# A later place for the value products and keys prepared by pairs, in a two-layer trunk with latent attention

## The chip, the cores and the metric

The kernel runs on one core of a Trainium2 chip. The metric is the device time of one execution in microseconds (us), as the median of several runs. The profile is that of one execution, taken by the hardware profiler; its times are counted from the first instruction of the program. Engines are called as the profile calls them: PE is TensorE's matmul and PEld its weight load, DVE is VectorE, ACT is ScalarE, POOL is GpSimd, and SP is the engine whose queue issues nearly all DMAs.

## The reference

The input is 512 tokens of 1024 channels, with 16 learned meta tokens put in front (528 rows in all). Two layers follow. Each normalizes the residual stream, projects it by one wide matrix into eight parts, and mixes tokens in two parallel ways: causal pooling over four windows, and attention with 8 heads. A head has 64 channels without position and 32 channels with rotary position (rope); the 32 rope channels of the key are the same for all heads before the key is normalized, and the norm then gives every head its own factor per token.

```python
q = (c_q @ w_q_b).reshape(B, L, N_HEADS, QK_HEAD_DIM)
kv = (c_kv @ w_kv_b).reshape(B, L, N_HEADS, QK_NOPE_DIM + V_HEAD_DIM)
k_nope, v = kv[..., :QK_NOPE_DIM], kv[..., QK_NOPE_DIM:]
k_pe = jnp.broadcast_to(k_rope_raw[:, :, None, :], (B, L, N_HEADS, QK_ROPE_DIM))
k = jnp.concatenate([k_nope, k_pe], axis=-1)
q = rmsnorm(q, g_qn)
k = rmsnorm(k, g_kn)
...
o = causal_block_attention(q, k, v)          # softmax(q k^T / sqrt(96)) v, causal
...
y_mla = (o_mla * jax.nn.silu(z_mla)) @ mla_w_up[l]
merged = jax.nn.sigmoid(g_pool) * y_pool + jax.nn.sigmoid(g_mla) * y_mla
h_res = h_res + merged @ w_out[l]
```

All is in float32, and the result has to hold float32 accuracy.

## The kernel before, in words

**Precision.** TensorE works on a shorter float32 form (fp32r). So each operand is split into a high part, which ScalarE makes by a copy (`act.activation(..., AF.Copy)`), and a low part, which VectorE makes by a subtraction. `split` (L294 to L296) does this for activations and `wload` (L196, L197) for weights. A product is three matmuls (L201 to L203): high by high, high by low, low by high.

**Two streams of work.** Activations are kept transposed, channels on partitions and the 528 tokens along the row. All weight products of both layers stand in one list, `plan`; `stream` (L210) walks it chunk by chunk (512 columns of weight, that is four tiles of 128 by 128) and yields after every six matmuls, with 6 x columns / 2.4 as its planned nanoseconds. Weights are loaded into `raw` (three buffers) by SP. The attention of a layer is written out by hand in `go` (L1084) and `head` (L784), and in its gaps `fill` (L282) draws from the stream as many planned nanoseconds as `FILL` says (2620 in layer 0, 2530 in layer 1), until `gm3` is done; the products gm4 to gm7 are kept for the end. `fill_now` draws a given amount at once, and `after` puts a piece of work (a closure) behind so many nanoseconds of drawn stream; `LAG` is 2000.

**Order of the work.** The framework plans at build time: it simulates a timeline (`schedule_with_timeline_sim=True`), takes for each engine the earliest piece in program order whose inputs are ready in the simulation, and so freezes one order per engine. On the chip each engine works its queue strictly in that order, and a DMA that has to wait stands in SP's queue ahead of all that follows. `behind` (L302) adds a true wait for another instruction; `newest` is the last matmul of the stream that has been written out.

**One head.** `prep(h)` makes the key and the query of a head. The key factors, one row per head in DRAM (`kdr`), were broadcast over 128 partitions by `spread_k` (L758), two heads ahead. VectorE multiplies 64 rows of the normalized key by them (L767), POOL the rope rows (L768), and `split` makes `kh` and `kl` (two buffers each). Even heads have their position-free rows on partitions 0 to 63 and rope on 64 to 95, odd heads have rope on 0 to 31 and the others on 64 to 127; the rest of the query is zero. The query's rope rows are copied into `qhl` by two DMAs (L781).

`head(h)` then computes scores of query tiles 1, 3 (in part) and 2 (L201 to L203 with output S), their row minimum on VectorE (L803), the exponentials on ScalarE (L810) and block transposes on VectorE (`turn`, L816). After a gap, `parts(prev)` splits the turned probabilities of the head before, and after another gap come the rest of tile 3 and tile 0 (L841), with the same steps. The transposed blocks go to DRAM by four DMAs (`pdr<-attD`, L868) and come back in order by one (`attE<-pdr`, L870; two buffers). The row sums go through DRAM too (L863, L871). For an odd head the 16 meta keys of two heads are turned and sent through DRAM into `racc` (L885, L887; one buffer).

`parts` (L890) splits `attE`: two activations of 128x640 into `th` and two subtractions in place. `pv` (L900) is the value product: four matmuls with the high part (L918) and four with the low part (L921) into one PSUM bank `o` (for the last head a bank of S), then ScalarE and VectorE add its two halves (L926, L927). For an odd head `part2` (L931) follows after two lags, for the last head after three: it adds the meta keys' part (L933), multiplies by the gate (L936, L937) and splits the result into `ogs`, from which the products mu0 to mu7 are made.

The loop over heads in `go` is: `head(h)`, gap, `prep(h+1)`, `pv` of head h-1, gap. After the loop come the meta tokens' own queries (layer 0), 2600 ns of stream, `parts` of head 7, 2600 ns more, its `pv`, and the rest of the stream up to `gm7`.

## Time and profile before

| what | value |
|---|---|
| median of 3 runs | 799.87 us (798.21 to 802.26) |
| the profiled execution, as timed | 800.05 us |
| its span, first to last instruction | 798.3 us |
| granted TensorE clock, mean over the span | 0.987 |
| busy: PE, DVE, ACT, POOL | 766.5, 553.7, 397.1, 166.4 us |
| heads of layer 0 and of layer 1, about | 172 to 326 us and 575 to 723 us |

A row of the groups reads: line, engine, operation, output<-inputs, partitions x elements and count, then busy time and the mean of one in ns, then the idle time of the engine just before and what ended it. A row of the waits reads: who waited, for whom, the total in us, how often, the longest. A row of a timeline or of the chain reads: start in us, length in us, engine, line. A row of an instruction group of one line has minimum, median and maximum in ns and the first and last start.

### The profile page before, as it was taken

The numbers are of one execution on the slowest core, as the hardware profiler recorded it, in microseconds if no ns is written. First come the engines' busy times: TensorE is split into PE (matmuls) and PEld (weight loads), VectorE is DVE, ScalarE is ACT, GpSimd is POOL, SyncE is SP. The second block draws the span as 40 slices with busy tenths as digits, with TensorE's granted clock in tenths as the row PEclk, the third lists the DMA queues.
The fourth block names the chain that finished last, engine by engine and source line by source line (L and its number), as shares of the span: only waits on it lengthen the run. The fifth ranks groups of instructions, "written<-read, shape, count | busy, mean of one in ns | idle before, by whom it ended". The sixth has DMA issues, their size and how long they took to land. (4 is left out here: it accounts for less than half of the span.)

```text
span 798.3 us, 14211 instructions
## 1 busy us (share of the span) xinstructions
PE 766.5 (96%) x5028; PEld 692.4 (87%) x5028; DVE 553.7 (69%) x1219; ACT 397.1 (50%) x868; POOL 166.4 (21%) x195
## 2 busy tenths in 40 slices
PE   9999999999898999999999999999998989889998
PEld 9999999999897998899997898887886767768887
DVE  5588677457788986684466486674567979868642
ACT  5755656445544654543354355564435555554321
POOL 2026204011112220052130262030112212211400
PEclk9999999999899999999999999999999999999999
DMA  7533233345555565424642332233455564573353
GB/s 266 170 103 103 69 100 107 96 142 160 163 157 165 150 172 171 124 99 141 182 137 92 109 93 78 96 96 118 148 165 152 143 190 145 158 222 121 106 185 105
DMA packets 74642, 109.76 MB, mean 138 GB/s; under 512 B 14358, under 2 KB 35222, under 8 KB 74572
## 3 DMA queue, kind: packets, MB, share of 16 engines
q1 hardware_dynamic: 74428, 108.61, 44.8%
q8 instruction: 39, 0.64, 0.3%
q14 instruction: 31, 0.25, 0.1%
q10 hardware_dynamic: 144, 0.26, 0.1%
HBM read 90.85 MB, written 15.86 MB: 134 GB/s over the span
## 5 line engine op out<-in xcount | busy, mean ns | idle before, releaser
L203 PE MATMUL mm<-hh,wlo 128*128 128x264 f32 (+2 forms) x1072 | 339.4, 319 | 3.5 <-DVE wlo L197 3.5
L201 PE MATMUL mm<-hh,whi 128*128 128x264 f32 (+2 forms) x1072 | 339.3, 318 | 0.8 <-ACT whi L196 0.8
L202 PE MATMUL mm<-hl,whi 128*128 128x264 f32 (+2 forms) x1072 | 338.6, 317 | 0.0
L197 DVE TENSOR_TENSOR wlo<-raw,whi 128x512 fp32r<-128x512 f32 (+2 forms) x242 | 175.0, 727 | 89.2 <-ACT whi L196 85.6
L196 ACT ACTIVATE whi<-raw 128x512 fp32r<-128x512 f32 (+2 forms) x242 | 144.1, 599 | 152.3 <-PE mm L202 124.3
L203 PEld LDWEIGHTS mm<-hh,wlo 128*128 128x128 f32 x1072 | 202.7, 190 | 17.2 <-DVE wlo L197 5.1
L201 PEld LDWEIGHTS mm<-hh,whi 128*128 128x128 f32 x1072 | 203.7, 190 | 14.7 <-ACT whi L196 1.3
L202 PEld LDWEIGHTS mm<-hl,whi 128*128 128x128 f32 x1072 | 203.6, 190 | 13.1
L296 DVE TENSOR_TENSOR attE<-attE,th 128x640 fp32r<-128x640 f32 x32 | 30.5, 972 | 39.8 <-ACT th L295 39.8
L295 ACT ACTIVATE th<-attE 128x640 fp32r<-128x640 f32 x32 | 21.9, 729 | 60.3 <-DMA attE<-pdr 60.3
L768 POOL TENSOR_TENSOR tmp<-kp,bc 64x528 f32<-64x528 f32 x16 | 25.5, 1592 | 85.3 <-PE mm L203 69.8
L813 POOL COPY pm<-cq 128x16 f32<-128x16 f32 x32 | 13.5, 423 | 141.4 <-ACT cq L810 140.6
L628 POOL TENSOR_TENSOR racc<-racc,tmp 128x264 f32<-128x264 f32 (+1 forms) x15 | 14.3, 957 | 135.3 <-ACT tmp L627 135.3
L803 DVE CUSTOM_DVE_ANT_0 S<-S,maskw,nqs 128x240 f32<-128x240 f32 (+4 forms) x80 | 37.6, 492 | 5.2 <-PE S L203 4.6
L993 POOL TENSOR_TENSOR tmp<-tmp,xb 128x264 f32<-128x264 f32 (+1 forms) x24 | 26.1, 1097 | 51.2 <-DVE tmp L991 45.9
L810 ACT ACTIVATE cq<-S,bia 128x400 f32<-128x400 f32 (+2 forms) x48 | 24.4, 511 | 21.8 <-DVE bia L803 14.1
L201 PE MATMUL mm<-cq,whi 128*128 128x264 f32 (+1 forms) x108 | 34.8, 322 | 0.0
L202 PE MATMUL mm<-th,whi 128*128 128x264 f32 (+1 forms) x108 | 34.6, 321 | 0.0
L201 PE MATMUL mm<-u,whi 128*128 128x264 f32 (+1 forms) x108 | 34.6, 320 | 0.0
L203 PE MATMUL mm<-cq,wlo 128*128 128x264 f32 (+1 forms) x108 | 34.5, 321 | 0.0
L202 PE MATMUL mm<-cq,whi 128*128 128x264 f32 (+1 forms) x108 | 34.5, 321 | 0.0
L203 PE MATMUL mm<-u,wlo 128*128 128x264 f32 (+1 forms) x108 | 34.5, 319 | 0.0
(295 smaller groups left out, 1334.5 us busy)
## 6 DMA issues: line engine op xcount, KB each, us to landing
raw<-win SPq DMA_DIRECT2D x143, 256.0 KB, 2.9
pdr<-attD SPq DMA_DIRECT2D x64, 160.0 KB, 3.0
attE<-pdr SPq DMA_DIRECT2D x16, 640.0 KB, 4.8
raw<-wout SPq DMA_DIRECT2D x32, 256.0 KB, 2.8
bc<-kdr SPq DMA_DIRECT2D x16, 264.0 KB, 3.7
raw<-wpu SPq DMA_DIRECT2D x16, 256.0 KB, 2.6
raw<-wmu SPq DMA_DIRECT2D x16, 256.0 KB, 2.6
raw<-wqb SPq DMA_DIRECT2D x12, 256.0 KB, 2.6
```

The lines of the kernel that those rows point to most:

```text
L196: act.activation(hi[:, :n], raw[:, :n], AF.Copy)
L197: dve.tensor_sub(lo[:, :n], raw[:, :n], hi[:, :n].bitcast(F32))
L201: first = pe.matmul(out, wh, xh, start=start, stop=False)
L202: pe.matmul(out, wh, xl, start=False, stop=False)
L203: newest[0] = pe.matmul(out, wl, xh, start=False, stop=stop)
L295: act.activation(hi[:, a:b], src, AF.Copy)
L296: return dve.tensor_sub(lo[:, a:b], src, hi[:, a:b].bitcast(F32))
L628: self.acc_last = gp.tensor_add(self.acc[:, a:b], self.acc[:, a:b], t[:, :b - a])
L768: gp.tensor_mul(kf[r0:r0 + 64, :], self.kp[r0:r0 + 64, :], bc[r0:r0 + 64, :])]
L803: return dve.tensor_tensor_reduce(out=sv, in0=sv, in1=mask, scale=nqs[:, i, h:h + 1], scalar=3e38, op0=ALU.add, op1=ALU.min, accum_out=bia ...
L810: act.activation(pv, sv, AF.Exp, scale=-1.0, bias=bia[:, i:i + 1], accum_out=rs[:, c:c + 1])
L993: gp.tensor_add(t[:, :b - a], t[:, :b - a], self.am[m][:, a:b])
```

## The change

It has four parts.

1. The value product of head h-1 moves from the end of the loop's pass h into the middle of `head(h+1)`, where `parts` was; `parts` of head h-1 moves to the end of pass h, after `prep(h+1)`. In the program `late` is the head whose parts are made and whose product is due, `prev` the one before that.
2. In `parts` the two high parts wait, by `behind`, for the stream's newest matmul at that place.
3. After the loop stand the product of head 6, then 9000 planned ns of stream (`TAIL`) instead of 2600, `parts` of head 7, 2600 ns and its product.
4. Keys: `keys(p)` multiplies and splits all 128 rows of a pair of heads at once, in the middle of the odd head before, with factors of two heads broadcast to 64 partitions each. The rope rows of four heads at a time are multiplied and split once per layer, in `k_factors`, for which the raw rope rows are copied to all four groups of 32 partitions in `kr_rest`. `prep` then puts a head's key together by DMA: the rope rows (two DMAs, for all heads) and, for even heads, the 64 position-free rows (two more) into the second buffer. The odd head's key is the pair's own buffer. Even heads use 96 partitions in the score products.

```diff
--- before.py
+++ after.py
@@ -53,6 +53,7 @@
 FILL = (2620.0, 2530.0)
 RESERVE = ("gm3", "gm3")
 LAG = 2000.0
+TAIL = (9000.0, 9000.0)
 SPL = 240
 RET = 12500.0
 WARM = 8
@@ -503,7 +504,8 @@
                 self.kraw = slot("kn3")
             t, kr = self.kp[:, a:b], self.kraw[:, a:b]
             behind(dve.tensor_mul(t, t, self.inv[:, a:b]), newest[0])
-            gp.tensor_copy(t[64:96, :], t[0:32, :])
+            for g in (32, 64, 96):
+                gp.tensor_copy(t[g:g + 32, :], t[0:32, :])
             q = next(self.half)
             made = act.activation(q[:, :b - a], t, AF.Square)
             self.stat(q[:, :b - a], a, b, C_KPE, made)
@@ -543,8 +545,17 @@
             newton(ny, na, nt)
             sp.dma_start(flat(kdr[self.l]), ny)
             self.bcs = {}
-            for h in range(2):
-                self.spread_k(h)
+            self.spread_k(0)
+            self.kr = []
+            for r in range(2):
+                bc = slot("bc", bufs=3)
+                sp.dma_start(bc, kdr[self.l][4 * r:4 * r + 4, :].unsqueeze(1).to_broadcast([4, 32, T]))
+                f = tmp()
+                dve.tensor_mul(f[:, :T], self.kp, bc)
+                t = slot(f"cq{4 + 2 * r}", F32R), slot(f"cq{5 + 2 * r}", F32R)
+                split(*t, f[:, :T], 0, T)
+                self.kr.append(t)
+            self.spread_k(1)
 
         def rope(self, out, src, a, b):
             n = b - a
@@ -753,33 +764,41 @@
                 self.smeta = self.smeta32[0:NM]
                 gp.memset(self.smeta32, 0.0)
 
-        def spread_k(self, h):
-            self.bcs[h] = bc = slot("bc", bufs=3)
-            sp.dma_start(bc, kdr[self.l][h:h + 1, :].partition_broadcast(P))
+        def spread_k(self, p):
+            self.bcs[p] = bc = slot("bc", bufs=3)
+            sp.dma_start(bc, kdr[self.l][2 * p:2 * p + 2, :].unsqueeze(1).to_broadcast([2, 64, T]))
+
+        def keys(self, p):
+            t = [(slot("kh", F32R, bufs=2), slot("kl", F32R, bufs=2)) for _ in range(2)]
+            self.ks[p] = t if p % 2 else t[::-1]
+            kf, bc = tmp()[:, :T], self.bcs.pop(p)
+            made = dve.tensor_mul(kf, self.kn[p], bc)
+            if p + 2 < H // 2:
+                self.spread_k(p + 2)
+            split(*self.ks[p][1], kf, 0, T)
+            return made
 
         def prep(self, h):
             p, odd = h // 2, h % 2
             n0, r0 = (64, 0) if odd else (0, 64)
-            kf = tmp()
-            bc = self.bcs.pop(h)
-            if h + 2 < H:
-                self.spread_k(h + 2)
-            made = [dve.tensor_mul(kf[n0:n0 + 64, :], self.kn[p][n0:n0 + 64, :], bc[n0:n0 + 64, :]),
-                    gp.tensor_mul(kf[r0:r0 + 64, :], self.kp[r0:r0 + 64, :], bc[r0:r0 + 64, :])]
-            kh, kl = slot("kh", F32R, bufs=2), slot("kl", F32R, bufs=2)
-            split(kh, kl, kf[:, :T], 0, T)
+            kd = self.ks[p][odd]
+            g0 = 32 * (h % 4)
             qh, ql = qhl[odd]
             x0 = self.x0
             src = self.qn[p][n0:n0 + 64, x0:T]
-            made.append(act.activation(qh[n0:n0 + 64, x0:T], src, AF.Copy))
+            made = act.activation(qh[n0:n0 + 64, x0:T], src, AF.Copy)
             if h == 0:
-                for ins in made:
-                    behind(ins, newest[0])
+                behind(made, newest[0])
             dve.tensor_sub(ql[n0:n0 + 64, x0:T], src, qh[n0:n0 + 64, x0:T].bitcast(F32))
-            g0 = 32 * (h % 4)
+            if odd == 0:
+                for d, f in zip(kd, self.ks[p][1]):
+                    sp.dma_start(d[0:64, :].bitcast(F32), f[0:64, :].bitcast(F32))
+            for d, f in zip(kd, self.kr[h // 4]):
+                sp.dma_start(d[r0:r0 + 32, :].bitcast(F32), f[g0:g0 + 32, :].bitcast(F32))
             for d, f in zip((qh, ql), self.qr[h // 4]):
                 sp.dma_start(d[r0:r0 + 32, x0:T].bitcast(F32), f[g0:g0 + 32, x0:T].bitcast(F32))
-            return kh, kl, qh, ql
+            m = P if odd else QK
+            return [t[0:m] for t in (*kd, qh, ql)]
 
         def head(self, h, kq, prev):
             kh, kl, qh, ql = kq
@@ -831,7 +850,9 @@
             turn(1)
             turn(2)
             self.gap()
-            self.parts(prev)
+            self.pv(prev)
+            if odd and h + 1 < H:
+                self.keys(h // 2 + 1)
             self.gap()
             sc = sct()
             s0, s4 = sc[:, 0:144], sc[:, 144:144 + T - SPL]
@@ -889,13 +910,14 @@
 
         def parts(self, prev):
             if prev is None:
-                return
+                return None
             h, got = prev
-            hi = wide()
-            f = got.bitcast(F32)
+            hi, f = wide(), got.bitcast(F32)
             for a in (0, NB * 64):
-                split(hi, got, f[:, a:a + NB * 64], a, a + NB * 64)
-            self.pt = hi, got
+                b = a + NB * 64
+                behind(act.activation(hi[:, a:b], f[:, a:b], AF.Copy), newest[0])
+                dve.tensor_sub(got[:, a:b], f[:, a:b], hi[:, a:b].bitcast(F32))
+            return h, hi, got
 
         def pv(self, prev, hosts=()):
             if prev is None:
@@ -914,7 +936,7 @@
             for j in range(4):
                 k0, n = block(j, j), 4 - j
                 st = block(j + 1, j) - k0 if n > 1 else 1
-                hi, lo = (t.rearrange("p (a s r) -> p s a r", a=4, s=NB)[:, k0:k0 + st * (n - 1) + 1:st] for t in self.pt)
+                hi, lo = (t.rearrange("p (a s r) -> p s a r", a=4, s=NB)[:, k0:k0 + st * (n - 1) + 1:st] for t in prev[1:])
                 chain(pe.matmul(o[:, P * j:512], vt[:, j, h, :], hi, start=j == 0, stop=j == 3))
                 for fn in hosts[2 * j:2 * j + 2]:
                     chain(fn())
@@ -1120,24 +1142,27 @@
             up("qn3")
             self.qk_stats()
             fill_now(2600)
+            self.ks = [None] * 4
+            behind(self.keys(0), newest[0])
             kq = self.prep(0)
             fill_now(2600)
             due[0] = None
-            prev = None
+            late = prev = None
             for h in range(H):
-                now = self.head(h, kq, prev)
+                now = self.head(h, kq, late)
                 self.gap()
                 if h + 1 < H:
                     kq = self.prep(h + 1)
-                self.pv(prev)
+                late = self.parts(prev)
                 prev = now
                 self.gap()
+            self.pv(late)
             if not self.last:
                 self.meta_queries()
+            fill_now(TAIL[self.l])
+            late = self.parts(prev)
             fill_now(2600)
-            self.parts(prev)
-            fill_now(2600)
-            self.pv(prev)
+            self.pv(late)
             up("gm7")
             flush()
             if not self.last:
```

## The prediction

> **What bounds the kernel now.** I read the page first, then TensorE's waits, then stretches of the two attention stages, then the chain that ended last. The page says that TensorE is the bound, with 798.3 - 766.5 = 31.8 us of idle time in the whole span:

> ```profile
> span 798.3 us, 14211 instructions
> ...
> PE 766.5 (96%) x5028; PEld 692.4 (87%) x5028; DVE 553.7 (69%) x1219; ACT 397.1 (50%) x868; POOL 166.4 (21%) x195
> ```

> The profiled execution took 800.05 us, so 1.75 us lie around the span; the median of the three runs is 799.87, 0.2 below it. The waits of TensorE (total, times, longest):

> ```profile
> PE o L918 <- ACT th L295: 15.7, 11, 3.6
> PE S L918 <- ACT th L295: 4.5, 2, 2.5
> PE mm L203 <- DVE wlo L197: 3.5, 4, 1.3
> PE mm L933 <- DMA racc<-mdr: 2.2, 2, 1.7
> ```

> So 15.7 + 4.5 = 20.2 us of idle time is the value product (L918) waiting for ScalarE's high part of the turned probabilities (L295). The next view has the attention stage of layer 0 and of layer 1, and below them the five stretches that follow the longest of these waits (columns: window; length and PE; PEld; DVE; ACT; POOL; granted clock; DMA share; GB/s):

> ```profile
> 172.00:326.00 154.00, 140.80 (x1075) 137.37 (x1075) 124.81 (x325) 79.58 (x202) 27.99 (x43) 0.96 0.54 159
> 575.00:723.00 148.00, 134.11 (x621) 107.15 (x620) 118.43 (x270) 75.56 (x176) 29.22 (x43) 0.98 0.58 164
> 216.50:222.30 5.80, 5.80 (x24) 5.51 (x25) 5.74 (x12) 3.75 (x12) 2.57 (x3) 0.50 0.18 58
> 259.90:263.30 3.40, 3.40 (x15) 3.00 (x14) 3.40 (x10) 2.16 (x9) 0.60 (x2) 0.50 0.33 100
> 321.30:324.70 3.40, 3.40 (x14) 3.30 (x15) 3.40 (x8) 1.60 (x5) 0.77 (x1) 0.50 0.13 48
> 618.30:621.70 3.40, 3.40 (x10) 2.51 (x9) 3.40 (x9) 2.05 (x6) 2.56 (x4) 0.50 0.30 79
> 717.30:720.70 3.40, 3.40 (x10) 2.42 (x9) 3.40 (x5) 1.61 (x4) 0.50 (x1) 0.51 0.20 58
> ```

> After five of the waits TensorE runs at half clock, busy all through, for 5.8 + 4 x 3.4 = 19.4 us. At full clock that work takes half: 9.7 us more are lost to these waits than the list of waits tells.

> Why the product waits: the probabilities go out to DRAM and back. The chain shows it for the last head (start, length):

> ```profile
> 706.06 0.32 SPq L868
> ...
> 707.39 3.56 DMA pdr<-attD
> 711.14 4.42 DMA attE<-pdr
> ...
> 716.23 0.73 ACT th L295
> 717.00 0.60 PE S L918
> ```

> ScalarE's own queue makes it worse. It reaches the split of the parts before the load has landed and stands there: 60.3 us in all, 3.8 a head, 7.1 at most. Behind it stand the exponentials of the next head:

> ```profile
> ACT th L295 <- DMA attE<-pdr: 60.3, 16, 7.1
> 215.03 1.36 ACT L295 ACTIVATE th<-attE 128x640 fp32r<-128x640 f32 x2 [5.42 <-DMA attE<-pdr]
> 217.98 0.44 ACT L810 ACTIVATE cq<-S,bia 128x240 f32<-128x240 f32 x1
> ```

> **The change, part by part.** *Later products.* In the program the parts of head h move from behind the first filler gap of head h+1 to behind its third, and its value product from behind that third gap to behind the first gap of head h+2: two gaps each. A gap is 2620 ns of the planner's time, four steps of 660. Its real length:

> ```profile
> 236.02 0.29 PE L201 MATMUL mm<-hh,whi 128*128 128x264 f32 x1
> 237.00 0.28 PE L203 MATMUL mm<-hh,wlo 128*128 128x264 f32 x1
> ```

> Eight matmuls take 0.98 us, so a step of six takes 0.74, a gap 2.9 and two gaps 5.9 us, plus the next head's scores for the product. ScalarE's mean wait of 3.8 us is covered, its longest of 7.1 nearly; the product's longest wait of 3.6 is covered. The head that is hardest to cover is head 3, whose product also stands late in TensorE's order: the last scores of the next head ended at 247.1 and the product came only at 258.7, 11.6 us later, where one gap (2.9) was meant, so it lacks 8.7 against a move of 5.9 plus scores. I take that as covered too, because ScalarE's idle 5.42 us ahead of the exponentials, which delay the next head's own probabilities, are to end with the change.

> ```profile
> 247.10 0.17 PE L841 MATMUL S<-kh,qhl 128*16 128x16 f32 x1
> 258.71 0.50 PE L918 MATMUL o<-th,vt 128*128 128x512 f32 x1 [2.57 <-ACT th L295]
> ```

> Gain: 20.2 of waits and 9.7 of clock. The 2.2 us for the meta part (L933) go too: it follows the product, 5.9 us later against a longest wait of 1.7. Neither step issues a DMA, but both hold buffers longer: the load of head h+2 into attE (two buffers) waits for the product of head h, which now stands in the middle of head h+2, two gaps ahead of that load; the meta load of the next odd head (L887, one buffer) waits for the meta product, 4000 ns of plan behind the value product and so still a gap ahead: 0 for both. Together 32.1. What is late next is VectorE's low part of weights (3.5 us today); I leave it as it is, bounds -3.5 and +12 (rival 2).

> *Parts held.* Both splits now also wait for TensorE's newest matmul at that place. Behind them in ScalarE's queue are weight splits and exponentials, for which TensorE and VectorE wait. The hold ends when TensorE gets there, which is where the program wants the work. It replaces idle time of ScalarE, which is busy 79.58 of 154 us. Cost taken 0; lower bound 0, upper bound the wait it replaces (rival 4).

> *Keys by pairs.* Rows of one key preparation:

> ```profile
> L767 DVE TENSOR_TENSOR tmp<-kn,bc x16: 690/704/1894, 168.9 to 681.6; 64x528 f32<-64x528 f32 x16
> L295 ACT ACTIVATE kh<-tmp x6: 630/638/647, 202.7 to 284.6; 128x528 fp32r<-128x528 f32 x6
> L296 DVE TENSOR_TENSOR kl<-tmp,kh x6: 664/694/1949, 204.3 to 286.2; 128x528 fp32r<-128x528 f32 x6
> L768 POOL TENSOR_TENSOR tmp<-kp,bc 64x528 f32<-64x528 f32 x16 | 25.5, 1592 | 85.3 <-PE mm L203 69.8
> L506 POOL COPY kp<-kp x4: 400/428/466, 60.5 to 461.5; 32x264 f32<-32x264 f32 x4
> ```

> Per layer VectorE did 8 x (0.70 + 0.69) = 11.1 us and does 4 pairs and 2 sets of rope rows, 8.3; ScalarE 8 x 0.64 becomes 6 x 0.64; POOL loses 8 x 1.59 and gains four copies of 0.43 long before the heads. All of it lies beside TensorE, so it counts 0, except as room: within the heads VectorE loses 5.6 us of 124.81.

> *New copies.* Per layer 8 broadcasts become 6, and 16 copies of rope rows and 8 of the even heads' 64 rows are added: 22 more DMAs. The nearest row is the same kind of copy, query rows; its issue takes 0.52 us on SP:

> ```profile
> L781 SPq DMA_DIRECT2D qhl<-q x32: 507/520/612, 129.3 to 671.3; - x32
> ...
> DMA to landing us min/median/max: 2.0/3.7/6.2
> 230.87 0.17 PE L841 MATMUL S<-kh,qhl 128*16 128x16 f32 x1
> 231.04 0.52 SPq L781 DMA_DIRECT2D qhl<-q  x1
> 238.49 0.29 PE L201 MATMUL S<-kh,qhl 128*128 128x272 f32 x1
> ```

> For odd heads the copies write rows that are free early: 0. For heads 2, 4 and 6 the copies write the buffer that the head before still reads, so they start after its last scores. Today a query copy starts 0.17 us after such scores. Six copies issued in a row, the last landing 3.7 us after its issue: 0.17 + 5 x 0.52 + 3.7 = 6.5 us. The next scores stand two gaps behind, 5.9 us (today 7.6 in the rows above, value product included). Wait: 0.6, taken as 0.7 for what queues on SP ahead of them (value stores, weight loads); six such places, 4.2 us. With the shortest landing it is 0; with the longest, 6.2, it is 9.0 - 5.9 = 3.1 each.

> [...]

> *First head.* Keys were ready at 172.59 and scores began at 173.29; now copies of about 1.6 + 3.7 us come between, against one gap that follows:

> ```profile
> 171.90 0.69 DVE L296 TENSOR_TENSOR kl<-tmp,kh 128x528 fp32r<-128x528 f32 x1
> 173.29 0.29 PE L201 MATMUL S<-kh,qhl 128*128 128x272 f32 x1
> ```

> Up to 5.3 - 2.9 = 2.4 us could show; later filler can step in, so 0.5 per layer, 1.0.

> *End of a layer.* 6400 ns more filler stand before the last product, so as much less behind it. Of 21 us planned behind the limit (four gm products of 5.28) 9.5 planned, 10.5 real, are left. What they must cover: three of the planner's lags (6.7 us real), then two VectorE operations of 0.69, a split of 0.64 + 0.69. That is 9.4:

> ```profile
> 328.73 0.68 DVE L936 TENSOR_TENSOR tmp<-mm,tmp 128x512 f32<-128x512 f32 x1
> ```

> It just fits: 0.5 per layer, 1.0, bounds 0 and 3 each.

> *Sum.* I leave one half-clock stretch, 1.7, since some wait over 2 us will remain. 800.05 - 20.2 - 9.7 - 2.2 + 4.2 + 1.0 + 1.0 + 1.7 = 775.9; less the 0.2 to the median, 775.7. With every new price at 0 and the weight waits gone too: 799.9 - 35.6 = 764.3.

> **The rivals.** *1, slower: the even heads' copies are late.* Without them the gain is 32.1 - 3.7 = 28.4. Each late copy costs its wait w and, from about 1.8 us on, a half-clock stretch of 1.7: 6 x (w + 1.7) passes 28.4 from w = 3.0. The longest landing gives 3.1, so it is not out of reach; if SP stands at a weight load first and w is 5, the time is 799.9 - 28.4 + 40.2 = 811.7. Against it: the median landing gives 0.6, and TensorE's order can be planned around it.

> *2: the wait moves to the weight split.* VectorE's share rises from 124.81 of 154 us (81%) to 119.2 of about 138 (86%). Four waits cost 3.5 us today, 0.9 each; one in each of 16 heads would be 14, so 10.5 more, with one more half-clock stretch: 788. Against it: the parts no longer press on VectorE at the moment they land.

> *3: the clock does not follow.* In layer 1 no wait of the product into o was over 1.8 us (the waits of that stage alone), and yet a stretch at half clock stands at 618.3:

> ```profile
> PE o L918 <- ACT th L295: 6.1, 5, 1.8
> ```

> If the half-clock stretches after the four shorter waits (at most 2.6 us) come from something else than those waits, 4 x 1.7 = 6.8 us stay: 782.5. For the waits speaks that each stretch starts at one. [...]

> *4: nothing moves.* The hold makes ScalarE wait as long for TensorE as it did for the load, and the chain shifts as a whole: 800.

> **How the numbers follow.** The forecast 0.57, rival 1 0.15, rival 2 0.17, rival 3 0.05, rival 4 0.06. The forecast, 2 and 3 are faster, 0.79; rival 4 is split between the same, 0.05, and slower, 0.01; with rival 1 slower has 0.16. Half a per cent, 4 us, is about what a measurement of this kernel tells from no change. The forecast's own range is 764 to 787; for 8 in 10 the range goes from 764.3 over rivals 2 and 3 up to 801, where rival 4 ends, and leaves out rival 1.

> **What the changed profile would show.** Right: the waits of L918 for L295 fall under 4 us, the wait of ScalarE for the load under 20, the granted clock of the attention stages is 0.99, POOL's 64x528 product is gone, and scores wait for the new copies some 4 us in all. Wrong: scores of heads 2, 4 and 6 wait 3 us and more and the clock halves there; or the weight split is waited for in most heads; or mu products wait for the last head.

## The result, and the profile after

The changed kernel takes 812.02 us (median of 4 runs, 810.08 to 813.06) against 800.13 for the kernel before (four runs, one more than above): the ratio is 1.0145, with a 95% interval of 1.0111 to 1.0179. It is 1.45% slower, a small loss but a clear one, as the whole interval lies above 1; 775.7 was forecast.

What was to go is gone. These are the longest waits of TensorE in the changed kernel (who waited for whom, total us, times, longest); the value product is L940 now, and it is not among them. The last row is ScalarE's wait for the turned probabilities, 60.3 us before:

```profile
PE S L202 <- DMA kh<-kh: 12.5, 1, 12.5
PE S L202 <- DMA kh<-cq: 11.0, 1, 11.0
PE mm L202 <- ACT xb L646: 6.7, 1, 6.7
PE mm L204 <- DVE wlo L198: 6.7, 1, 6.7
PE mm L202 <- DVE tmp L652: 2.4, 1, 2.4
...
ACT th L918 <- DMA attE<-pdr: 0.6, 1, 0.6
```

Four pauses, each once, take 12.5 + 11.0 + 6.7 + 6.7 = 36.9 us. All four lie ahead of the first head: two in layer 0 and two in layer 1. The next view gives stretches of the changed kernel (window; length and PE; PEld; DVE; ACT; POOL; granted clock; DMA share; GB/s). The first two rows are the time around the first head of each layer; the next four are what TensorE does right after each pause; the last is most of the heads of layer 0:

```profile
169.00:200.00 31.00, 11.81 (x63) 11.38 (x61) 7.00 (x11) 6.04 (x13) 0.00 (x0) 0.62 0.30 93
570.00:613.00 43.00, 25.26 (x95) 20.41 (x94) 12.45 (x26) 9.79 (x18) 0.20 (x1) 0.77 0.32 100
...
177.50:183.30 5.80, 5.80 (x26) 5.80 (x27) 5.35 (x9) 3.97 (x9) 0.00 (x0) 0.50 0.27 84
197.10:200.40 3.30, 3.30 (x14) 3.30 (x15) 0.69 (x1) 0.00 (x0) 0.00 (x0) 0.50 0.47 135
588.60:592.90 4.30, 4.30 (x10) 3.43 (x11) 4.18 (x7) 2.67 (x5) 0.00 (x0) 0.50 0.31 94
607.20:613.40 6.20, 6.20 (x21) 5.72 (x22) 2.46 (x8) 1.58 (x4) 0.20 (x1) 0.50 0.47 153
...
205.00:345.00 140.00, 135.57 (x1072) 133.18 (x1071) 111.79 (x307) 78.03 (x197) 14.62 (x34) 0.99 0.62 179
```

In the kernel before, the same first two windows had TensorE busy for 30.73 and 40.71 us at full clock. After the pauses it runs at half clock for 5.8 + 3.3 + 4.3 + 6.2 = 19.6 us, which loses 9.8. So 36.9 + 9.8 = 46.7 us are new, and the 32.1 of the prediction are gone: 798.3 - 32.1 + 46.7 = 812.9, where the span is 811.3. Left out on both sides are the wait of 2.4 us in the heads, with one more half-clock stretch behind it (285.7 to 289.1, 1.7 us lost), and 4.3 us of waits for weight splits that are gone (3.5 + 0.8). In the heads themselves the stage is what was forecast: TensorE is busy 97% at a clock of 0.99 (before, 91% at 0.96).

What TensorE waits for stands in the chain of the changed kernel (start, length), here from the pause in layer 0:

```profile
163.91 14.01 DMA bc<-kdr
...
178.57 0.70 DVE cq L297
...
180.41 0.70 DVE tmp L775
...
182.37 4.92 SPq L797
...
187.33 9.70 DMA kh<-kh
...
197.07 0.93 PE S L202 x2
```

The broadcast of rope factors takes 14.0 us, where a broadcast of the same 264 KB took 3.7 before. Then SP needs 4.92 us to issue one copy (0.52 for a query copy before), and the copy of 64 key rows lands 9.70 us after its issue. In stretches of this time the 16 DMA engines are mostly idle, at a share of 0.13. Windows of the changed kernel show it in their last two columns, the DMA share and GB/s:

```profile
174.00:178.00 4.00, 0.54 (x2) 0.54 (x3) 0.76 (x2) 1.44 (x3) 0.00 (x0) 0.50 0.13 50
178.00:182.00 4.00, 4.00 (x20) 4.00 (x19) 4.00 (x7) 3.10 (x8) 0.00 (x0) 0.50 0.13 49
...
192.00:197.00 5.00, 0.00 (x0) 0.00 (x0) 0.00 (x0) 0.00 (x0) 0.00 (x0) 0.50 0.13 46
```

A share of 0.13 is what two of 16 DMA engines give when they are busy all through (0.125); at 46 to 50 GB/s that is 23 to 25 GB/s each. And two is the leading count of the pair broadcast (the outermost number of the description that the DMA is given): it reads two rows and repeats each 64 times.

### The profile page after: what moved, and what is told of

The parts are those of the page before. It is cut to its first block, busy times and chain, and to the rows that moved or that the text cites. A ratio compares the mean times of both kernels' runs of the same rounds, so it can differ in the third digit from the quotient of the medians.

```text
span 811.3 us, 14267 instructions
## 1 busy us (share of the span) xinstructions
PE 764.8 (94%) x5028; PEld 694.8 (86%) x5028; DVE 535.9 (66%) x1211; ACT 393.4 (48%) x864; POOL 140.5 (17%) x187
## 4 chain that ended last, share of the span: by engine, by line
PE 79%; DMA 11%; DVE 5%; SPq 2%; issue 2%; ACT 1%; DVEq 0%; ACTq 0%
PE mm L202 24%; PE mm L204 24%; PE mm L203 23%; DMA bc<-kdr 3%; PE S L202 2%; DMA kh<-cq 2%; PE S L203 2%; PE S L204 2%; DMA kh<-kh 1%; DMA pdr<-attD 1%; DMA raw<-win 1%; DVE wlo L198 1%; DMA attE<-pdr 1%; SPq L797 1%; PE S L528 1%
## 5 line engine op out<-in xcount | busy, mean ns | idle before, releaser
L203 PE MATMUL mm<-hl,whi 128*128 128x264 f32 (+2 forms) x1072 | 339.7, 318 | 0.0
L197 ACT ACTIVATE whi<-raw 128x512 fp32r<-128x512 f32 (+2 forms) x242 | 144.4, 600 | 200.9 <-PE mm L203 121.9
L203 PEld LDWEIGHTS mm<-hl,whi 128*128 128x128 f32 x1072 | 204.4, 191 | 12.5
L832 POOL COPY pm<-cq 128x16 f32<-128x16 f32 x32 | 11.0, 344 | 259.9 <-ACT cq L829 259.9
L202 PE MATMUL S<-kh,qhl 96*128 96x272 f32 (+4 forms) x64 | 20.1, 328 | 26.1 <-DMA kh<-kh 12.5
L822 DVE CUSTOM_DVE_ANT_0 S<-S,maskw,nqs 128x272 f32<-128x272 f32 (+4 forms) x80 | 38.2, 500 | 5.3 <-PE S L204 3.6
L202 PEld LDWEIGHTS S<-kh,qhl 96*128 96x128 f32 (+1 forms) x64 | 12.6, 202 | 28.6 <-DMA kh<-kh 12.7
L203 PE MATMUL mm<-th,whi 128*128 128x264 f32 (+1 forms) x108 | 35.3, 327 | 0.0
L203 PE MATMUL mm<-cq,whi 128*128 128x264 f32 (+1 forms) x108 | 34.5, 321 | 0.0
L835 DVE STREAM_TRANSPOSE attD<-cq 128x256 f32<-128x256 f32 (+2 forms) x48 | 21.5, 473 | 18.4 <-DMA pdr<-attD 11.6
```

The lines of the kernel that those rows point to most:

```text
L197: act.activation(hi[:, :n], raw[:, :n], AF.Copy)
L202: first = pe.matmul(out, wh, xh, start=start, stop=False)
L203: pe.matmul(out, wh, xl, start=False, stop=False)
L822: return dve.tensor_tensor_reduce(out=sv, in0=sv, in1=mask, scale=nqs[:, i, h:h + 1], scalar=3e38, op0=ALU.add, op1=ALU.min, accum_out=bia ...
L832: gp.tensor_copy(pm[:, i, 16 * odd:16 * odd + 16], pt[i][:, 0:NM])
L835: dve.transpose(grid[:, :, k:k + n, :].rearrange("p b s r -> p s b r"), pt[i][:, NM + P * j:NM + P * (j + n)])
```

## The experiments

**Theory 1:** a DMA whose leading count is 2 or 4 runs on 2 or 4 of the 16 DMA engines; four such broadcasts stand ahead of the first head, and every load that is spread over all 16 queues behind them. **Theory 2:** the chain ahead of the first head is simply longer (factors, products, splits, copies). **Theory 3:** later products cost something of their own.

### Broadcasts row by row

```diff
-                sp.dma_start(bc, kdr[self.l][4 * r:4 * r + 4, :].unsqueeze(1).to_broadcast([4, 32, T]))
+                for g in range(4):
+                    sp.dma_start(bc[32 * g:32 * g + 32, :], kdr[self.l][4 * r + g:4 * r + g + 1, :].partition_broadcast(32))
...
-            sp.dma_start(bc, kdr[self.l][2 * p:2 * p + 2, :].unsqueeze(1).to_broadcast([2, 64, T]))
+            for g in range(2):
+                sp.dma_start(bc[64 * g:64 * g + 64, :], kdr[self.l][2 * p + g:2 * p + g + 1, :].partition_broadcast(64))
```

> The changed kernel with one edit: each broadcast of key factors is issued row by row (four DMAs of one row to 32 partitions, two of one row to 64) instead of one DMA from four or two rows. Theory 1 (a DMA whose outermost dimension is 4 or 2 runs on 4 or 2 of the 16 DMA engines, and everything queued on those engines stands behind it): TensorE's two pauses ahead of the first head of each layer (6.7 + 12.5 and 6.7 + 11.0 = 36.9 us) shrink to under 6 us together and the half-clock time with them (9.9 us): 766 to 774 us. Theory 2 (the longer chain ahead of the first head, factors, products, splits, copies, is what costs): at most 5 us better than the change, 807 to 812 us.

Measured: 767.35 us, ratio to the kernel before 0.9607 (0.9561 to 0.9652). The chain ahead of the first head is the same, with more DMAs, and it costs next to nothing: theory 2 falls. TensorE's longest waits of this kernel:

```profile
PE S L202 <- ACT cq L831: 2.1, 2, 1.0
PE mm L202 <- DVE tmp L653: 1.9, 1, 1.9
PE mm L202 <- ACT whi L197: 1.2, 1, 1.2
PE S L202 <- DMA kh<-kh: 1.1, 2, 0.7
...
PE S L202 <- DMA kh<-cq: 0.7, 1, 0.7
```

This version beats both kernels. The broadcasts of one row to 32 partitions land in 2.1 us here (2.4 at most).

### Which of the broadcasts

The first edit of the two above alone (rope factors by row, pairs still from two rows):

> The changed kernel with row-by-row broadcasts for the rope factors alone; the pair factors still come from two rows in one DMA. Theory 1: between the two, 780 to 800 us, and in the stretch where TensorE still pauses the DMA share is about 2/16 = 0.13. Theory 2: 807 to 812 us.

Measured: 809.04 us, 1.012 (1.0066 to 1.0173). Theory 1's range of 780 to 800 was missed: mending the rope factors gains almost nothing. The chain of this kernel shows why; of its DMAs, in order:

```profile
163.19 8.09 DMA bc<-kdr
172.80 9.11 DMA raw<-win
183.19 12.13 DMA kh<-kh
```

A weight load, which takes 2.9 us in the median of the kernel before, takes 9.11 behind a pair broadcast, and the copy of key rows 12.13. TensorE's pause for that copy ends at 195.5, and late in it the DMA share is the 0.13 that was expected:

```profile
190.00:192.00 2.00, 0.00 (x0) 0.00 (x0) 0.00 (x0) 0.00 (x0) 0.00 (x0) 0.50 0.13 50
```

The two-row broadcasts alone hold up what follows them. The size of the part was wrong, not its kind, and the converse run says the same (pairs by row, rope factors still from four rows):

> The changed kernel with row-by-row broadcasts for the pair factors alone; the rope factors still come from four rows in one DMA. Theory 1: four engines at 23 GB/s each take 2.9 us a broadcast, two of them 5.9, against some 4 by row, so the first head starts a few us later: 767 to 775 us. If any source of several rows were slow, it would be near the change: 800 us or more.

Measured: 772.57 us, 0.9645 (0.96 to 0.969). VectorE waits 15.5 us in all for the four-row rope factors of both layers, against 3.5 by row, but the time is 772.57 us against 767.35, with intervals that overlap.

### The description alone, on the kernel before

To have nothing else in it, the old kernel's broadcast of one row got another description of the same bytes; once with 2 blocks of 64 copies, once with 16 blocks of 8. The two programs have the same instructions in the same order on all five engines.

```diff
-            sp.dma_start(bc, kdr[self.l][h:h + 1, :].partition_broadcast(P))
+            src = kdr[self.l][h:h + 1, :]
+            sp.dma_start(bc, src.unsqueeze(1).to_broadcast([1, 64, T]).to_broadcast([2, 64, T]))
```

> The kernel before with one edit: each broadcast of a key row to 128 partitions is described as 2 blocks of 64 copies instead of 128 copies of one row; same bytes, same source, same order of every engine as before_sixteen. Theory 1 (the leading count of the DMA's description is the number of DMA engines it runs on): 264 KB at the 46 GB/s that two engines moved in the changed kernel take 5.9 us instead of about 2, the three ahead of the first head 17.7 us, and weight loads stand behind them: 815 to 840 us. Rival (it was the change's longer chain or its four source rows, not the split over DMA engines): 797 to 803 us.

> The same edit with 16 blocks of 8 copies. Theory 1: all 16 DMA engines, 796 to 803 us as before. If a nested description alone costs, it is as slow as before_two.

Measured: 843.56 us with 2 blocks, 1.0528 (1.0474 to 1.0581); 801.47 with 16, 1.0016 (0.9991 to 1.004). The first lies a little beyond its range; its expectation took a broadcast over 16 engines at about 2 us, which no run shows: the kernel before has 3.7, and the one with 16 blocks 4.2. A leading count of 2 instead of 16 costs some 42 us with the same 109.76 MB and the same 14211 instructions. The DMA packets differ by 224 (74418 against 74642), 14 for each of the 16 broadcasts, the difference of 16 and 2. The same stretch in both kernels, first with 2 blocks:

```profile
178.00:182.00 4.00, 0.00 (x0) 0.00 (x0) 0.00 (x0) 0.00 (x0) 0.00 (x0) 0.50 0.13 50
```

and then with 16:

```profile
178.00:182.00 4.00, 4.00 (x37) 4.00 (x36) 3.48 (x12) 2.33 (x5) 1.33 (x2) 1.00 0.32 99
```

No compute engine works in the first, and the DMA share is again 0.13, about 2/16. SP, too, is held up; its own timeline with 2 blocks shows three broadcasts taking 4.64 us to issue and three weight loads 7.13:

```profile
162.43 4.64 SPq L759 DMA_DIRECT2D bc<-kdr  x3
167.12 7.13 SPq L132 DMA_DIRECT2D raw<-win  x3
```

With 16 blocks the three broadcasts took 1.85 and the three loads behind them 3.85. So theory 1 is borne out for a count of 2, with a share of 0.13 of 16 engines both for two rows and for 2 blocks of one row. The share at a count of 4 by itself, and what sets the number of engines, are not shown.

### Later products alone, keys alone

The change taken apart. Later products, hold and longer tail on the old keys, and the new keys with products and parts in their old places:

> The kernel before with later products, held parts and the longer tail alone; keys are prepared as before. Theory 1: the waits for parts (20.2 us) and their half clock (9.7) go and nothing comes in their place: 767 to 773 us. Rival (later products cost as much as they bring, by the hold or at the end of a layer): 795 us or more.

> The changed kernel with parts and products in their old places and no hold: the new keys alone. Theory 1: the loss ahead of the first heads (36.9 + 9.9 us) comes on top of the time before, 840 to 850 us, and the waits of the product for its parts are there as before, 15 to 22 us. Rival (later products cost): 812 us or less.

Measured: 772.3 us, 0.9673 (0.9615 to 0.9731), and 844.49 us, 1.0563 (1.0511 to 1.0616). Both as theory 1 has it, and theory 3 falls. The whole loss is in the new keys, and with row-by-row broadcasts it is gone from them:

> The new keys with row-by-row broadcasts, parts and products in their old places, no hold. If the new keys bring nothing of weight by themselves: the waits of the product remain, 15 to 25 us, 788 to 803 us. If the room they give VectorE and POOL is what shortens the stage: 785 us or less.

Measured: 794.6 us, 0.9937 (0.991 to 0.9963). The keys bring a little by themselves; the product's waits are there as before (16.1 + 6.5 us).

### Hold or later place

Row-by-row broadcasts and later products, but without the hold:

```diff
-                behind(act.activation(hi[:, a:b], f[:, a:b], AF.Copy), newest[0])
+                act.activation(hi[:, a:b], f[:, a:b], AF.Copy)
```

> The changed kernel with row-by-row broadcasts and without the hold on the parts. If the hold is what keeps ScalarE from standing at a load that has not landed, ScalarE's waits for that load rise over 20 us and the time goes to 775 to 790 us. If the later place alone does it: 765 to 770 us.

Measured: 802.77 us, 1.0015 (0.9984 to 1.0045). The hold is worth more than was expected: without it the gain is gone altogether. Its waits, of ScalarE for the load:

```profile
ACT th L920 <- DMA attE<-pdr: 71.6, 15, 7.2
```

and of TensorE:

```profile
PE S L202 <- ACT cq L831: 19.9, 9, 5.2
```

The product no longer waits for its parts in o. But ScalarE still reaches the parts before their load has landed. ScalarE's own order shows it at the first parts. Without the hold they stand ahead of the exponentials (L831):

```profile
196.66 1.37 ACT L920 ACTIVATE th<-attE 128x640 fp32r<-128x640 f32 x2 [4.63 <-DMA attE<-pdr]
...
202.44 0.46 ACT L831 ACTIVATE cq<-S,bia 128x240 f32<-128x240 f32 x1 [1.94 <-DVE bia L877]
```

and with it, in the kernel with all broadcasts by row, right behind them:

```profile
197.59 0.38 ACT L831 ACTIVATE pa<-S,bia 128x144 f32<-128x144 f32 x1
...
197.94 1.36 ACT L920 ACTIVATE th<-attE 128x640 fp32r<-128x640 f32 x2
```

So the planner had set the parts early again. The likely reason, that ScalarE has time there in the planner's simulation, is not shown by a run. With the exponentials late the score banks are not freed, and now it is the next scores that wait. The same hold in the old place, with old keys and old products:

> The kernel before with the hold alone: parts in their old place, waiting for the stream's newest matmul there; products and keys as before. If hold and later place are both needed: at the old place the load has not landed, so the product goes on waiting for its parts, 15 us or more in all, 788 to 805 us. If the hold alone is the gain: 780 us or less.

Measured: 799.08 us, 0.9997 (0.9978 to 1.0016): nothing. And the later place on the old keys without the hold:

> The kernel before with later products and the longer tail, keys as before, parts not held. With it the four corners of hold and later place stand on the old keys. If only both together bring the gain: 793 to 805 us, ScalarE waiting 60 us or more for the load. If the later place alone does it where the keys are the old ones: 767 to 778 us.

Measured: 796.18 us, 0.9893 (0.9845 to 0.994); ScalarE waits 56.1 us for the load, a little under the 60 that were expected. So neither part brings the gain alone:

| ratio to the kernel before | old keys | new keys, by row |
|---|---|---|
| neither | 1 | 0.9937 |
| hold alone | 0.9997 | not run |
| later place alone | 0.9893 | 1.0015 |
| both | 0.9673 | 0.9607 |

The intervals of the two in the last row overlap, so what the new keys add to later products is not settled.

### The longer tail

```diff
-TAIL = (9000.0, 9000.0)
+TAIL = (2600.0, 2600.0)
```

> Row-by-row broadcasts and the rest of the change, with 2600 ns of stream ahead of the last head's parts instead of 9000. If the longer tail is needed to cover the last load: the last product waits some 2 to 4 us for its parts in each layer and the clock halves once behind it, 771 to 780 us. If not: 765 to 770 us.

Measured: 768.11 us, 0.9613 (0.9576 to 0.9649), where 771 to 780 was expected for a tail that matters. One wait of 1.8 us for the last parts comes back, and in the time nothing shows:

```profile
PE S L942 <- ACT th L920: 1.8, 1, 1.8
```

## Why the prediction was wrong

**Later products: near in size, and the reason was half of it.** Alone, with the hold, they bring 25.9 us (798.16 to 772.3), where 32.1 was counted; there 4.8 us of the product's waits are left. In the whole change the 20.2 us of waits, the clock that followed them and the meta part's 2.2 are gone. But the prediction put this down to the two gaps by which the work moves, and priced the hold at 0. The runs show that the move alone brings 0.9893 or nothing and that both are needed. The prediction quoted the row that tells it, ScalarE standing 5.42 us ahead of exponentials, and did not draw that the planner would set the parts as early in the new place.

**Keys by pairs as room only:** 0 was taken; by row the new keys alone are at 0.9937, some 5 us. Near enough.

**New copies for heads 2, 4 and 6:** 4.2 us were taken. In the changed kernel scores behind the first heads wait for a key copy once, 0.9 us. With row-by-row broadcasts all waits of scores for key copies are 1.1 + 0.7 = 1.8 us, and 1.4 of them lie at the first heads. So rival 1, whose time of 811.7 is so near the measured one, did not happen; that its number fits is chance.

**First head: the step that failed.** "8 broadcasts become 6" was counted as DMAs of the kind that the trace knew, with a landing of 3.7 us; their own time ahead of the first head was put at nothing, and the lateness of the first head was put at 0.5 us a layer with 2.4 at most. Measured were 6.7 + 12.5 and 6.7 + 11.0 us of pauses, and 9.8 us of half clock. The diff holds what the runs then tied the loss to: the two broadcasts have leading counts of 4 and 2, the old one had 128. An estimate shows the size. By the rate of the trace after, two DMA engines (a share of 0.13) move 46 to 50 GB/s. Ahead of the rope factors they have, if a count of 4 means four engines, as theory 1 has it, and they are also among the four, half of 264 KB from the pair broadcast and a quarter of it from each of two rope broadcasts, 132 KB each on the two engines, 264 in all: about 5.6 us for the pair broadcast, and as much again for the two rope ones. That is 11.2 us, and some 2 us to land (2.1 for one row to 32 partitions in the row-by-row kernel), where the chain has 14.0. With the broadcasts by row the first heads wait 0.7 us in each layer, close to the 0.5 that the prediction took.

**End of a layer:** 1.0 us was taken; the tail makes no measurable difference, 0.9613 against 0.9607.

**The sum without the failed term:** 775.7 was forecast and 767.35 measured with the broadcasts by row. The unchanged kernel was at 798.16 in that session, 1.7 us under the sum's start. The copies of heads 2, 4 and 6 cost some 0.4 us instead of 4.2, and the waits for weight splits fell from 4.3 us to 1.2, where the sum had left them as they were. Together these are 1.7 + 3.8 + 3.1 = 8.6 us, about the whole. The one half-clock stretch that the sum left is there, after a wait of 1.9 us:

```profile
260.00:263.40 3.40, 3.40 (x18) 3.40 (x17) 3.34 (x11) 2.27 (x9) 0.39 (x2) 0.51 0.63 159
```

**The other rivals.** The wait on weight splits in most heads (rival 2) did not come: in the row-by-row kernel TensorE waits for one once, 1.2 us for a high part (whi). The clock did follow the waits (rival 3): it is 0.998 over that kernel's span, against 0.987 before. Rival 4, that nothing moves, blamed the hold. The runs show the reverse: without the hold nothing moves (802.77), and with it the time falls to 767.35. None of the three signs that the prediction named for being wrong came: all three look at the heads or behind them, and the loss lies ahead of the first head.

## What to carry to other kernels

Read the leading count of every new or changed DMA before pricing it by its bytes: here the kernel took 809.04 us with the pair broadcasts from two rows in one DMA and 767.35 with two broadcasts of one row each, and what was queued behind the two-row ones was late (a weight load landed after 9.11 us instead of 2.9). When a planner fills an idle engine's queue early, moving work to a later place in the program need not move it in the queue; it needs something that keeps it there. And when a change is slower, take it apart before dropping it: here one DMA description hid a gain of 4%.

## What was not expected of the hardware

The same bytes cost 42 us more by their description alone (843.56 against 801.47 us). Broadcasts with a leading count of 2 held up the DMAs behind them: with the rope factors by row and the pairs from two rows, a weight load landed after 9.11 us instead of 2.9. In the changed kernel the issuing queue itself stood for 4.92 us at one copy, where a query copy before took 0.52. And the clock halved after a wait of at most 1.8 us (layer 1 of the kernel before).

The traces say more on this. In those of the kernel before and of the changed kernel every stretch at one clock, the last of a run apart, lasts 3.41 us or a multiple of it: before, the five at half clock last 6.83 us once and 3.41 four times, and the shortest at full clock 37.55, eleven times 3.41. So in these two traces the clock changed in steps of 3.41 us. Three such steps of the kernel before:

```profile
614.85:618.26 3.41, 1.65 (x7) 1.04 (x6) 1.22 (x1) 1.99 (x4) 1.44 (x1) 1.00 0.82 294
618.26:621.68 3.42, 3.42 (x10) 2.53 (x9) 3.42 (x9) 2.09 (x6) 2.60 (x4) 0.50 0.31 81
696.76:700.17 3.41, 1.74 (x11) 1.41 (x9) 3.29 (x8) 1.88 (x6) 1.40 (x4) 1.00 0.71 172
```
